# RWKV strips first with block 0's inverse among the other strips, and the GLA heads placed beside block 0's steps

## The chip, the cores and the metric

The kernel runs on one core of a Trainium2 chip. The metric is the device time of one execution in microseconds; a lower time is better. One profiled execution of each kernel gives the trace, in which PE is the matmul engine, DVE, ACT and POOL are the vector, scalar and GpSimd engines, and SP issues most transfers.

## The reference

One block of a diffusion model on 512 latent tokens and 256 context tokens of width 1024. One projection (w_in, 3328 columns) feeds two groups of heads: RWKV-7 (8 heads of 64, both directions) and gated linear attention, GLA (4 heads, both directions). Their outputs go through one projection w_out; an expert-choice mixture of 16 experts follows.

```
proj = h @ w_in
z_rw, z_gla = proj[..., :RW_IN], proj[..., RW_IN:]
z_rw = z_rw + delta_fn(z_rw) * rw_mu                  # token shift: neighbours in the sequence or grid
r, k, v, wd_f, wd_b, ad_f, ad_b, gd = split(z_rw)
g_out = sigmoid(gd) @ rw_g2
y, s = wkv7_scan(r, decay, kk, kk * a, k, v, s0)      # per direction; s <- s*w - (s.kk) kka + v k
rw_out = (group_norm(y_f + y_b) + bonus) * g_out
q, kg, vg, gg, gad_f, gad_b = split(z_gla)
log_a = log_sigmoid(gad @ gla_a2 + gla_a_b) / 16
o = gla_chunked(q, kg, vg, log_a, s0)                 # chunks of 64: b = cumsum(log_a),
                                                      # q*exp(b), k*exp(-b), one state from chunk to chunk
gla_out = rmsnorm(o_f + o_b) * gla_norm_w * silu(gg)
x = ln(ALPHA * x + g1 * (concat(rw_out, gla_out) @ w_out))
x = ln(ALPHA * x + g2 * expert_choice_ffn(modulate(ln(x)), router_w, w_gate, w_up, w_down))
```

## The kernel before

The work is written as Python generators and calls; a scheduler fixes from them, by priorities, one order for each engine, and each engine runs its instructions in that order. Waits on other engines and on transfers are semaphores.

**The strips.** `strip` loads 128 columns of w_in (L287, 512 KB) into one of two buffers `raw`, ACT copies it to `wh` (L289), POOL takes the rest into `wl` (L290). `project` (L298) multiplies with the tokens, three products for each of eight slices of the width (`wh` with `hh`, `wl` with `hh`, `wh` with `hl`). `shifted` adds the token shift. There are 26 strips: gates and GLA keys, queries, values first, then the low-rank strip LT, then blocks of RWKV (k, v and r of a block of two heads; four blocks, 0 to 3).

**GLA.** Per direction and half the decay is computed (L506 to L524). Then 11 chunk steps, each with transposes of the keys (L573, by L45), a copy `kt` (L575), the products with the values (L580) and the state on DVE (L590 to L593). Then scores (L606) and outputs (L627) of eight chunks, four normed heads (L641 to L650) and their write to `og_d` (L651). `feed` hands out strips between the steps.

**Parking w_out.** `park` takes w_out in 16 tiles: a load into `wx` (L554), the product with g1 on DVE (L555), a rounded copy on ACT (L556), the rest on POOL (L557), a write to `wo_d` (L558). `wx` has three buffers, and `ox`, from which the heads are written, has the same tag t3.

**RWKV per block.** `rw_elem` makes the elementwise terms (e_c, e_w, e_i, e_t, matmuls L689, L707, L708); `rw_keys` fills KB and AM (L747 to L751), `rw_scores` multiplies them (L842), `rw_inverse` inverts a triangular matrix for each chunk and head: QD (L866), 15 substitution steps on DVE (L884, L887), block products (L899 to L934), copies into SC (L948, L949). `rw_rho` is L762, `clear` L778. Then 12 steps `rw_step`: the copy of `wt` (L987) on DVE comes once in each step, which needs the state of the step ahead. `rw_post` norms a block's output.

**The order of the blocks before.** All strips and the GLA (53 to 374 us), with block 0's elementwise terms among them. Then scores and inverse of block 0 with `gla_half` (the 96 products L1094 of the GLA heads with their part of w_out, operands `mxg` from `og_d` and `wg` from `wo_d`, loaded on POOL's queue) and block 1's elementwise terms in its gaps. Then block 0's steps, with keys, scores and inverse of block 1 beside them, and so on with the next block. In the first part PSUM has banks d, s and c; behind it w, k, e, i and u.

## Time and profile before

| what | us |
|---|---|
| median of 3 runs (lowest, highest) | 2104.27 (2096.83, 2109.34) |
| the profiled execution, its span | 2105.25, 2103.5 |
| PE busy, DVE, ACT, POOL over the span | 1831.6, 769.4, 481.1, 315.7 |
| strips and GLA | 53 to 374 |
| inverse of block 0, products of the GLA heads | 374 to 437 |
| block 0's steps, keys to inverse of block 1 | 437 to 534 |
| experts | 794 to the end |

The stages are read from the trace; the busy times are of the page. An engine's busy share over the span mixes stages, so the section with rows below cuts the span into windows. A row of a timeline names the start, the duration, the engine, the line, the operation with its tiles, and in brackets the idle time ahead and what ended it.

### The profile page before, as it was taken

Reading aid. Unit: us, or ns where it says so; the run is one execution under the profiler, and the core shown is the slowest. Engines: PE = TensorE matmul, PEld = TensorE weight load, DVE = VectorE, ACT = ScalarE, POOL = GpSimd, SP = SyncE. Lnnn points to the kernel's source line nnn. Section 1 sums busy time; section 2 is a strip of 40 time slices with the busy share of each in tenths; the row PEclk is TensorE's granted clock in tenths of the full one; section 3 lists DMA queues with packets and bytes.
Section 4 is the critical chain, followed back from the end, with each engine's and each line's share of the span. In section 5 each row is a group of like instructions: output and inputs, shape, how many; then the busy total and the mean of one; then the engine's idle time right before and its main releaser. Section 6 shows DMA issues by size and latency. Waiting matters only on the chain. (4 is left out here: it accounts for less than half of the span.)

```text
span 2103.5 us, 31329 instructions
## 1 busy us (share of the span) xinstructions
PE 1831.6 (87%) x13266; PEld 936.1 (44%) x13266; DVE 769.4 (37%) x1445; ACT 481.1 (23%) x978; POOL 315.7 (15%) x318
## 2 busy tenths in 40 slices
PE   5898997788889988999998888988988888889886
PEld 1666776666667653333333333333333332333322
DVE  4676667766663262122112112122122121121113
ACT  2242445555652441011101101010010010011001
POOL 2543656343140220000000000000000000000001
PEclk8989998888897999999999999999999999999998
DMA  7645631510000268999999999999999999999995
GB/s 276 180 147 184 216 102 45 174 46 18 2 28 7 87 269 371 424 424 425 425 425 424 425 425 425 424 425 425 425 425 424 424 425 424 425 424 424 426 424 226
DMA packets 111416, 638.50 MB, mean 304 GB/s; under 512 B 13007, under 2 KB 40248, under 8 KB 60332
## 3 DMA queue, kind: packets, MB, share of 16 engines
q1 hardware_dynamic: 108944, 625.74, 73.1%
q0 software_dynamic: 2016, 10.49, 1.5%
q8 instruction: 104, 1.70, 0.3%
q10 hardware_dynamic: 316, 0.28, 0.0%
q14 instruction: 36, 0.29, 0.0%
HBM read 619.54 MB, written 15.75 MB: 302 GB/s over the span
## 5 line engine op out<-in xcount | busy, mean ns | idle before, releaser
L1446 PE MATMUL ps_gu<-wt,xT 128*64 128x512 f32 (+1 forms) x3072 | 689.2, 568 | 47.7 <-DMA wt<-in_ex_up_dram 35.7
L1446 PEld LDWEIGHTS ps_gu<-wt,xT 128*64 128x64 f32 x3072 | 239.2, 138 | 435.3 <-issue 292.4
L1494 PE MATMUL ps_gu<-wd,hT 128*64 128x512 f32 x1408 | 311.4, 595 | 31.6 <-DMA wd<-in_ex_down_dram 31.6
L1494 PEld LDWEIGHTS ps_gu<-wd,hT 128*64 128x64 f32 x1408 | 97.3, 137 | 233.8 <-issue 173.2
L1467 ACT ACTIVATE gT<-ps_m 128x512 f32<-128x512 f32 x16 | 9.6, 597 | 602.1 <-PE ps_m L45 602.1
L1508 DVE TENSOR_TENSOR ye<-ps_gu,g2b 128x512 f32<-128x512 f32 x16 | 11.1, 692 | 372.1 <-PE ps_gu L1494 372.1
L1297 POOL MEMSET cnt<- 128x12 f32 x16 | 1.6, 107 | 884.8 <-DVE rank L1319 872.7
L1409 PE MATMUL ps_m<-h,oh 128*64 128x512 f32 x256 | 93.1, 615 | 45.9 <-DVE oh L1404 45.9
L1520 DVE TENSOR_TENSOR kx<-kx,ps_m 128x512 f32<-128x512 f32 x120 | 77.1, 684 | 152.0 <-PE ps_m L1514 152.0
L298 PE MATMUL ps_d<-hh,wh 128*128 128x512 f32 (+1 forms) x336 | 127.3, 379 | 4.2 <-ACT kx L362 3.0
L298 PE MATMUL ps_d<-hh,wl 128*128 128x512 f32 (+1 forms) x336 | 122.5, 365 | 5.3 <-POOL wl L290 5.3
L298 PE MATMUL ps_d<-hl,wh 128*128 128x512 f32 (+1 forms) x336 | 123.6, 368 | 3.4 <-POOL hl L269 3.4
L88 DVE TENSOR_SCALAR hm<-hm 128x512 f32<-128x512 f32 (+1 forms) x48 | 19.5, 405 | 180.6 <-ACT hm L1458 180.6
L1411 ACT ACTIVATE xg<-ps_m 128x512 f32<-128x512 f32 x16 | 9.6, 597 | 330.1 <-PE ps_m L1409 330.1
L290 POOL TENSOR_TENSOR wl<-raw,wh 128x1024 fp32r<-128x1024 f32 x26 | 67.4, 2592 | 93.7 <-ACT wh L289 92.8
L1418 DVE TENSOR_TENSOR xT<-ps_m,mod 128x512 f32<-128x512 f32 x16 | 11.1, 692 | 188.5 <-PE ps_m L1414 188.5
L298 PEld LDWEIGHTS ps_d<-hh,wh 128*128 128x128 f32 x336 | 66.9, 199 | 25.8 <-issue 10.1
L298 PEld LDWEIGHTS ps_d<-hh,wl 128*128 128x128 f32 x336 | 67.2, 200 | 15.1 <-POOL wl L290 5.5
L298 PEld LDWEIGHTS ps_d<-hl,wh 128*128 128x128 f32 x336 | 66.9, 199 | 14.3 <-POOL hl L269 5.1
L1514 PE MATMUL ps_m<-ye,gT 64*128 64x512 f32 x244 | 68.8, 640 | 0.0
L1409 PEld LDWEIGHTS ps_m<-h,oh 128*64 128x64 f32 x256 | 28.9, 142 | 85.4 <-issue 77.6
L1303 DVE SCALAR_TENSOR_TENSOR scr<-ps_m,aff,lo 128x128 bf16<-128x128 f32 (+3 forms) x60 | 33.1, 551 | 91.6 <-PE ps_m L1399 90.0
(454 smaller groups left out, 2669.8 us busy)
## 6 DMA issues: line engine op xcount, KB each, us to landing
wt<-in_ex_gate_dram SPq DMA_DIRECT2D x128, 1408.0 KB, 26.4
wt<-in_ex_up_dram SPq DMA_DIRECT2D x128, 1408.0 KB, 27.1
wd<-in_ex_down_dram SPq DMA_DIRECT2D x96, 1536.0 KB, 27.6
wd<-in_ex_down_dram SPq DMA_DIRECT2D x32, 1024.0 KB
adat<-in_ada_w_dram SPq DMA_DIRECT2D x64, 256.0 KB, 3.0
raw<-in_w_in_dram SPq DMA_DIRECT2D x25, 512.0 KB, 3.8
adat<-in_ada_w_dram SPq DMA_DIRECT2D x4, 2048.0 KB
wo_d<-wx SPq DMA_DIRECT2D x16, 512.0 KB, 3.8
```

Of the source, the lines that this page charges most:

```text
L88: V.tensor_scalar(o, o, 1.0, 2.0 ** 60, op0=A, op1=OP.min)
L290: G.tensor_tensor(wl, raw, wh.bitcast(F32), op=S_)
L298: mm(p, a[:, k, :], b[:, k, lo:lo + n], start=k + i == 0, stop=k == KD - 1 and i == 2)
L1303: V.scalar_tensor_tensor(scr[:, l:h], row[:, l:h], aff[:, t, e:e + 1], (lo if before else hi)[:, z + l:z + h], op0=OP.is_ge if before else ...
L1409: mm(p[HR[h]], oh[:, t], h2[t][:, 512 * h:512 * h + 512], start=t == 0, stop=t == 3, skip_group_check=True)
L1411: act(xg, p, AF.Copy)
L1418: V.tensor_tensor(xv, p.rearrange("p (j h s) -> p j h s", j=4, h=2), sc, op=M)
L1446: i = mm(p[HR[h]], xT[:, k], wt[:, h * FH + f0:h * FH + f0 + w], start=k == 0, stop=k == KD - 1, skip_group_check=True)
L1494: mm(py[HR[c]], hT[:, j0 + j, 64 * h:64 * h + 64], wts[h][:, j, 512 * c:512 * c + 512], start=j0 + j + h == 0, stop=j0 + j == 10 and h == ...
L1508: V.tensor_tensor(ye, py, g2b, op=M)
L1514: mm(ps_[c], gT[HR[c], t * P:(t + 1) * P], ye[HR[c]], start=not last, stop=True, skip_group_check=True)
L1520: V.tensor_tensor(x, x, ps_[c], op=A)
```

## The change

- LT's strip comes first, then k, v and r of block 0, then gates, k, v, r of block 1, GLA keys, queries, values and output gates, and k, v, r of blocks 2 and 3. Block 0's elementwise terms, keys, scores and inverse are written among these strips, with banks s and c in place of e and i.
- What the GLA needs (its gate inputs, q, k, v, output gates) and the strips of blocks 2 and 3 are written to DRAM (`zgl_d`, `zq_d`, `zkg_d`, `vg_d`, `sg_d`, `z_d`) and read back later.
- Block 1's elementwise terms, block 0's steps, and the GLA with the parking of w_out are then written one behind the other, and `gla_half` behind these. The GLA's banks are all of kind i, which has two. `wx` and `ox` have two buffers instead of three; g1 has one buffer, loaded anew for each four tiles.
- Keys to inverse of block 1 come behind `gla_half`; the buffers of odd blocks lie where `gla_half` had its tiles.
- `sht`, a buffer of the token shift, is single. Buffers of the steps (wt, VU, kbt, S, SP, sr) get a pool of their own.

The core of the diff:

```diff
+    cur = dict(d=lambda: bank("d", 2), s=lambda: bank("s", 3), c=lambda: bank("c", 3))
+    pd, pss, pc, pe, pi = (lambda n=n: cur[n]() for n in "dscei")
+    cur.update(e=cur["s"], i=cur["c"])
...
     def strips():
+        w = strip([(1536, P)])
+        yield from shifted(w, 12, LT, TC, 0)
...
+        done.add("lora")
+        for n in ("k0", "v0", "r0"):
+            yield from rw_strip(n, dict(k=zk, v=zv, r=zr)[n[0]][0])
...
+        for n in ("k1", "v1", "r1"):
+            yield from rw_strip(n, dict(k=zk, v=zv, r=zr)[n[0]][1])
...
+            q(zkg_d[:, i], z)
...
+        for i, n in enumerate(("k2", "v2", "r2", "k3", "v3", "r3")):
+            z = next(slot)
+            yield from rw_strip(n, z)
+            n = TL if n[0] == "r" else TT
+            nc.sync.dma_start(z_d[:, i, 0:n], z[:, 0:n])
+        done.add("all")
...
+    e = rw_elem(0, pe, fill)
+    for _ in rest:
+        pass
...
+    buffers(0, rpb)
+    rw_keys(0, *e)
+    PC = rw_prep(0, e)
+    until("all")
...
+    cur.update(e=lambda: bankr("e", 2), i=lambda: bankr("i", 2), s=lambda: bankr("i", 2), c=lambda: bankr("i", 2))
...
         def park():
-    wx = gp.tile([P, 3, 2, 512], F32, name="wx", tag="t3")
+            wx = gp.tile([P, 2, 2, 512], F32, name="wx", tag="t3")
...
+                g1 = gp.tile([P, 512], F32, name="g1", tag="ga2")
+                nc.sync.dma_start(g1, mod_d[0, c:c + 1].to_broadcast([P, 512]))
...
-    oxs = gp.tile([P, 3, 2, TL], F32, name="ox", tag="t3")
+        oxs = gp.tile([P, 2, 2, TL], F32, name="ox", tag="t3")
...
-    with after(sub[0]) if O("ea", 1) else contextlib.nullcontext():
-        e = rw_elem(1, pe)
+    e = rw_elem(1, pe)
+    steps(0, PC)
+    gla()
+    c_r2, rp = pool("rw2", "left")
+    late.append(rp)
     with H("glah"):
         gla_half()
     c_rc, rc = pool("rwc", "right")
-    buffers(1)
-    for b in range(4):
-        S = None
-        for s in range(12):
-            S = rw_step(b, s, S, PC)
+    buffers(1, rc)
...
+    for b in range(1, 4):
+        rw_keys(b, *e)
+        PC = rw_prep(b, e)
         if b < 3:
-            rw_keys(b + 1, *e)
-            PC = rw_prep(b + 1, e)
-        if b < 2:
-            e = rw_elem(b + 2, pe)
-        if b == 1:
+            e = rw_elem(b + 1, pe)
+        if b == 2:
             zgs = zp0.tile([P, 3, TL], F32, name="zgs", tag="zkv0")
...
+        steps(b, PC)
```

How this moves instructions, at the places where the prediction has its terms. In after, scores are L650, the inverse L676 to L767, a step's copy of `wt` L1012, the GLA's states L916 to L919, its outputs L953, the sums of squares L968, the parking L883 to L887, the heads' write L976, the products L1106. (A number behind a tile's name counts buffers.)

PE before, from the last strip on: block 0's scores (L842), then products of the GLA heads (L1094) with block 1's elementwise matmuls (L689, L707, L708) and the first of the inverse.

```order
L842 MATMUL ps_e<-AM_2369,KB_2368 128x128 x12
L842 MATMUL ps_e<-AM_2371,KB_2370 128x128 x12
L767 MATMUL ps_e<-e_c,bd_113 128x512
L689 MATMUL ps_e<-e_c,bd_113 128x256
L689 MATMUL ps_e<-e_c,bd_113 128x512
L1094 MATMUL ps_k<-wg,mxg 128x512 x42
L707 MATMUL ps_e<-LS,e_ws 128x256
L708 MATMUL ps_e<-LS,e_ws 128x256
L1094 MATMUL ps_k<-wg,mxg 128x512 x2
L707 MATMUL ps_e<-LS,e_ws 128x512
L1094 MATMUL ps_k<-wg,mxg 128x512
L708 MATMUL ps_e<-LS,e_ws 128x512
```

PE in after, behind the GLA: its last outputs, the heads, all 96 products in a piece (L1106), then block 1's first transposes.

```order
L953 MATMUL ps_i<-qin_3308,sg_3315 128x64 x2
L953 MATMUL ps_i<-zqa,kx_3312 128x64 x2
L968 MATMUL ps_i<-gt,on_3320 128x512 x4
L1106 MATMUL ps_k<-wg,mxg 128x512 x96
L45 MATMUL ps_k<-ident,kx_463 64x128 x4
L994 MATMUL ps_k<-ident,KB_4118 128x128 x2
L994 MATMUL ps_k<-ident,KB_4124 128x128 x2
```

The products left the stage of an inverse and stand by themselves, and block 1's keys and scores follow them.

PE in after, in the middle of the strips: block 0's scores.

```order
L298 MATMUL ps_d<-hh,wh_184 128x512
L298 MATMUL ps_d<-hh,wl_186 128x512
L650 MATMUL ps_s<-AM_1283,KB_1282 128x128 x12
L650 MATMUL ps_s<-AM_1289,KB_1288 128x128 x12
L610 MATMUL ps_s<-e_c,bd_125 128x512
L298 MATMUL ps_d<-hl,wh_184 128x512
L298 MATMUL ps_d<-hh,wh_184 128x512
L298 MATMUL ps_d<-hh,wl_186 128x512
```

Scores (and behind them the inverse) stand between matmuls of strips, where before they came after the last strip.

DVE in after, at the last two steps of block 0 (`wt` is copied once a step) with the first of the parking (L884) and of the GLA's states.

```order
L1042 SCALAR_TENSOR_TENSOR S<-ps_u,PC,SP 128x64 x2
L1072 TENSOR_TENSOR ym<-ym,ps_k 128x2x64
L884 TENSOR_TENSOR wx<-wx,g_3683 128x512
L1012 COPY wt<-ps_w 128x128
L916 TENSOR_TENSOR sg_3314<-ps_i,ebl 128x512
L1072 TENSOR_TENSOR ym<-ym,ps_k 128x2x64
L918 TENSOR_TENSOR sg_3315<-ps_i,sg_3314 128x512
L919 TENSOR_TENSOR sg_3315<-sg_3315,ebl 128x512
L918 TENSOR_TENSOR sg_3315<-ps_i,sg_3315 128x512
L884 TENSOR_TENSOR wx<-wx,g_3683 128x512
L919 TENSOR_TENSOR sg_3315<-sg_3315,ebl 128x512
L884 TENSOR_TENSOR wx<-wx,g_3683 128x512
```

DVE in after, from the last parking products to block 1's keys (L583).

```order
L884 TENSOR_TENSOR wx<-wx,g_3785 128x512
L972 SCALAR_TENSOR_TENSOR og<-gg,cols,gt 128x512 x2
L884 TENSOR_TENSOR wx<-wx,g_3785 128x512 x2
L975 TENSOR_TENSOR ox<-og,ox 128x512 x4
L1135 SCALAR_TENSOR_TENSOR xr<-xr,ps_k 128x512 x8
L583 TENSOR_TENSOR KB_4118<-e_c,e_i 128x12x64
```

Before, all of the parking and the GLA stood ahead of block 0's first copy of `wt`; now 14 of the 16 products of the parking stand behind its last one, ahead of `ox`, and the keys of block 1 behind that.

SP before, the parking's transfers with strips (`raw`) among them.

```order
L558 DMA wo_d<-wx 128x1024 x3
L554 DMA wx<-in_w_out_dram 128x512 x2
L287 DMA raw_174<-in_w_in_dram 128x8x128
L554 DMA wx<-in_w_out_dram 128x512
L558 DMA wo_d<-wx 128x1024 x3
```

SP in after, the same transfers.

```order
L887 DMA wo_d<-wx 128x1024 x2
L883 DMA wx<-in_w_out_dram 128x512 x2
L887 DMA wo_d<-wx 128x1024 x2
L879 DMA g_3717<-mod_d 128x512
L883 DMA wx<-in_w_out_dram 128x512 x2
```

Three writes in a row became two, and no strip stands among them.

## Rows read from the trace of the kernel before

**Rows 1.** Windows: us, busy of each engine with instructions, granted clock, DMA share, GB/s.

```profile
53.00:374.00 321.00, 283.13 (x1795) 219.43 (x1795) 225.75 (x241) 132.95 (x213) 163.71 (x104) 0.93 0.45 143
374.00:437.00 63.00, 51.47 (x844) 39.83 (x843) 40.54 (x74) 36.87 (x53) 19.06 (x22) 0.89 0.50 170
437.00:534.00 97.00, 82.81 (x1442) 64.51 (x1443) 64.70 (x127) 52.03 (x121) 38.17 (x44) 0.83 0.06 18
794.00:2103.00 1309.00, 1150.16 (x5564) 432.95 (x5564) 277.39 (x603) 121.46 (x252) 19.21 (x32) 0.99 0.99 416
```

**Rows 2.** Timeline of PE: start, us, engine, line, instruction; at 73 and 375 us.

```profile
73.19 0.40 PE L298 MATMUL ps_d<-hh,wh 128*128 128x512 f32 x1
73.42 0.40 PE L298 MATMUL ps_d<-hh,wl 128*128 128x512 f32 x1
...
375.36 0.82 PE L842 MATMUL ps_e<-AM,KB 128*128 128x128 f32 x5 [0.42 <-ACT kx L362]
```

**Rows 3.** Page, section 5, over the span: busy us, mean ns, idle before.

```profile
L298 PE MATMUL ps_d<-hh,wl 128*128 128x512 f32 (+1 forms) x336 | 122.5, 365 | 5.3 <-POOL wl L290 5.3
```

**Rows 4.** Timeline of DVE at 480 and 534 us.

```profile
479.46 0.29 DVE L987 COPY wt<-ps_w 128x128 f32<-128x128 f32 x1 [0.16 <-PE ps_w L984]
483.75 0.29 DVE L987 COPY wt<-ps_w 128x128 f32<-128x128 f32 x1 [0.20 <-PE ps_w L984]
...
534.11 0.29 DVE L987 COPY wt<-ps_w 128x128 f32<-128x128 f32 x1
```

**Rows 5.** Windows, 185 to 312 us, of L45, L580, L606 and L627 alone.

```profile
185.00:312.00 127.00, 7.75 (x176) 6.49 (x176) 0.97 0.47 158
185.00:312.00 127.00, 12.65 (x176) 10.09 (x176) 0.97 0.47 158
185.00:312.00 127.00, 4.82 (x128) 4.29 (x128) 0.97 0.47 158
185.00:312.00 127.00, 13.73 (x192) 11.80 (x192) 0.97 0.47 158
```

**Rows 6.** Tile wx: ns min/median/max of one, first and last start.

```profile
L555 DVE TENSOR_TENSOR wx<-wx,g x16: 678/686/1780, 198.2 to 258.0; 128x512 f32<-128x512 f32 x16
L556 ACT ACTIVATE wx<-wx x16: 621/632/635, 199.0 to 259.3; 128x512 fp32r<-128x512 f32 x16
L557 POOL TENSOR_TENSOR wx<-wx x16: 1262/1516/1742, 199.7 to 260.6; 128x512 fp32r<-128x512 f32 x16
...
DMA to landing us min/median/max: 2.6/3.7/5.0
```

**Rows 7.** Page, section 6: DMA issues, KB each, us to landing.

```profile
wo_d<-wx SPq DMA_DIRECT2D x16, 512.0 KB, 3.8
```

**Rows 8.** Timeline of SP around 201 and 212 us.

```profile
201.30 3.25 SPq L558 DMA_DIRECT2D wo_d<-wx  x3
...
212.32 5.03 SPq L558 DMA_DIRECT2D wo_d<-wx  x3
```

**Rows 9.** Lines L641 (first step of a head) and L651 (its write).

```profile
L641 ACT ACTIVATE gt<-og x4: 613/626/632, 293.0 to 301.4; 128x512 f32<-128x512 f32 x4
...
L651 SPq DMA_DIRECT2D og_d<-ox x4: 320/332/345, 301.1 to 308.6; - x4
```

**Rows 10.** Tile mxg, its loads.

```profile
DMA to landing us min/median/max: 5.4/7.3/9.1
```

**Rows 11.** Groups by line, 185 to 312 us, as page section 5.

```profile
L580 PE MATMUL ps_c<-vg,kt 64*64 64x128 f32 x176 | 12.7, 288 | 4.3 <-ACT kt L575 4.2
```

**Rows 12.** Timeline of POOL, keys of block 1.

```profile
436.64 1.79 POOL L747 TENSOR_TENSOR AM<-e_c,e_w 64x756 f32<-64x756 f32 x1 [12.00 <-PE ps_k L1094]
...
449.34 5.58 POOL L762 TENSOR_TENSOR RM<-zr,e_w 64x512 f32<-64x512 f32 x4
```

**Rows 13.** Timeline of ACT, end of inverse 0.

```profile
434.76 0.37 ACT L949 ACTIVATE SC<-ps_i 32x256 f32<-32x256 f32 x1
```

**Rows 14.** Windows, DVE alone, behind block 1's second step.

```profile
534.00:603.00 69.00, 50.45 (x109) 0.94 0.07 21
```

More of the change, by code (lines that the diff above doesn't have):

```diff
@@ L860, in rw_inverse_ @@
         dg = lambda g: SC[j][1 - g // 2][R[g], :, 32 * (g % 2):32 * (g % 2) + 32]
-        QD = rp.tile([P, 32, 32], F32, name="QD", tag="X")
+        if b:
+            QD = late[1].tile([P, 32, 32], F32, name="QD", tag="X")
+        else:
+            QD = rpa.tile([P, 1536], F32, name="QD", tag="e_i")[:, 0:1024].rearrange("p (a b) -> p a b", b=32)
+            big = {n: rpa.tile([P, 1536], F32, name=f"x_{n}", tag=f"e_{n}") for n in "tcw"}
         G.memset(QD[:, :, 24:32], 0.0)
@@ L866, in rw_inverse_ @@
             act(o, i, AF.Copy)
-        gt = kp2.tile([P, 1056], F32, name="gt")
+        gt = late[1].tile([P, 1056], F32, name="gt") if b else big["t"][:, 0:1056]
         g3 = gt[:, 0:1024].rearrange("p (a b) -> p a b", b=32)
@@ L871, in rw_inverse_ @@
         busy(gt[:, 0:32], O("b1",(0,0))[b>0])
-        X = rp.tile([P, 1056], F32, name="X")
+        X = late[1].tile([P, 1056], F32, name="X") if b else rpa.tile([P, 1536], F32, name="X", tag="e_i")[:, 0:1056]
         G.memset(X, 0.0)
@@ L880, in rw_inverse_ @@
                 n, m = 15 - s, s + 1
[L881 removed]
+                tmp = late[1].tile([P, 128], F32, name="xtmp", bufs=1) if b else big["t"][:, 1056:1184]
                 tv = tmp[:, 0:2 * n * m].rearrange("p (i a b) -> p i a b", i=2, b=m)
```

579 lines of the change are left out of this document (285 added, 294 removed).

## The prediction

> **What bounds the kernel now.** I first cut the span at the places where the kind of work changes and read the busy time of each engine there [rows 1]. The last 1309 us, the experts, move 416 GB/s with the DMA engines 0.99 busy, and the change touches nothing there. All that it moves lies between 53 and 603 us. From 53 to 374 us PE is busy 283.1 of 321 us with the strips and the GLA: at their densest the strips' matmuls, 512 wide, stand 0.23 us apart [rows 2], and the granted clock is 0.93. The idle is 38 us in all, of it 5.3 us ahead of matmuls that wait for a strip's split on POOL [rows 3]. From 374 to 437 us the bound is another: the inverse of block 0 is a chain of small steps over four engines, and its gaps hold the 96 GLA products and block 1's elementwise work. From 437 to 534 us block 0's steps (4.3 us each where nothing is in the way [rows 4]) run beside the inverse of block 1; 534.1 us is block 1's second step, which needs that inverse. From block 1's steps on the order of after is that of before, so I take the time from there to the end as it is, and ask when block 1's second step comes.
>
> **The strips, 53 to 374 us.** Out go the GLA chain and outputs, 7.75 + 12.65 + 4.82 + 13.73 = 39 us of PE [rows 5], and the sums of squares of the four heads (4). In come scores, rho and inverse of block 0. Their PE work is bounded by the stage in which they now stand, 51.5 us busy [rows 1] less 96 products at 0.23, so at most 29; block 1's elementwise matmuls are among that too, and I take 17. Busy then is 283 - 43 + 17 = 257. Idle was 38; the inverse's small matmuls stand in order among the strips' and can hold them up, but some 400 matmuls follow it with nothing in the way, and the waits of the GLA chain are gone: 21. That makes 278, against 321, a gain of 43 us; its bounds are 252 (all idle gone) and 300 (idle and lost clock as now, and some 5 of new stalls). The some twenty new writes to DRAM (GLA inputs, late strips) go beside this, with the DMA share at 0.45 [rows 1], and cost nothing as long as that holds; if not, they are in the upper bound.
>
> **The stage 374 to 437 us falls out of the way ahead of block 0's steps.** That is what the change buys: at 53 + 278 = 331 us the first step can begin. Beside the steps stand now elementwise work of block 1 and the gates, by my sum over the order of after, with the durations that the same instructions have in the trace, some 47 us of DVE and 51 of ACT; twelve free steps take 52. I take 60 (52 to 68), so they end at 391.
>
> **What now stands behind block 0's steps.** This is the term that decides. In the order of DVE two of the 16 parking products (L884) and the first GLA state stand ahead of block 0's last copy of wt; the 14 others, ten GLA states, the outputs and the heads stand behind it. Four chains hang on each other there.
> - Parking. One tile is a load, a DVE product (0.69), an ACT copy (0.63), a POOL subtraction (1.5) and a write; a load lands after 3.7 us [rows 6], a write after 3.8 [rows 7], and the queue of the writes shows rounds of three buffers 11 to 12 us apart [rows 8]. With two buffers a round (the two buffers' loads, work and writes in a row on SP's queue) is 3.7 + 0.7 + 0.6 + 1.5 + 3.8 = 10.3 at the least, with the second tile's POOL 11.8; I take 11. The first pair's products stand some 6 us before the last step ends, so the eighth pair's are at -6 + 7 x 11 = +71 us after the steps, and its writes have landed at +78.
> - The heads. ox takes the buffer of wx (one of the tag t3), so its first ACT copy waits for the last write of the parking. Before, four heads followed each other in 293.0 to 308.6 us [rows 9]; their squares, roots and products with the gate now hide behind the parking, and what is left is two pairs of copy, subtraction, write: 2 x (2 + 3.8) = 12, so og_d is whole at +90.
> - The products. mxg and wg are loaded behind that on POOL's queue and landed after 7.3 us (5.4 to 9.1) [rows 10]; the 96 products then come in one piece, 96 x 0.233 = 22.4, since nothing of an inverse is left to pair them with. Before, the same 96 lay in the gaps of inverse 0 and cost that stage little. End: +90 + 7.3 + 22.4 = +120.
> - The GLA chain itself is 39 us of PE, and 45 with waits like the 4.2 us for kt that it had before [rows 11]; it hides beside the parking.
>
> I take 120, so 391 + 120 = 511. Bounds: 130 with rounds of 12.4, and 94 if the parking bounded nothing (45 + 15.6 for the heads + 3.8 for the last write + 7.3 + 22.4).
>
> The Trainium skill (DMA: Bandwidth & Descriptors, Anatomy of one DMA — SWDGE (gpsimd) path) gives a DMA of POOL's queue a fixed 2 us and the bytes at 436 GB/s; an estimate by that page for one of the loads of 1 MB is 4.4 us, and the sum would be 3 us less. The row says 7.3, for loads that share the engines, and the sum goes by the row.
>
> **Keys, scores and inverse of block 1.** Their buffers lie where the products' tiles are, so they begin behind them. Before, POOL's part (AM, clearing, RM) took 436.6 to 454.9 us [rows 12], 18 us, with nothing else needing it soon; now the scores wait for the AM part of it. From inverse 0's first scores (375.4 [rows 2]) to its last copy (434.8 + 0.4 [rows 13]) are 60 us, with elementwise work beside it as now. 18 + 60 = 78, and 2 for the keys, scores and elementwise work of block 2 that stand among them: 80 (68 if the scores start before POOL is through, 97 if it runs as inverse 1 did before, from 454.9 to 534). Block 1's second step is then at 511 + 80 = 591, where it was 534.1: +57. In the 69 us behind it DVE was busy 50.5 [rows 14]; elementwise work, keys and scores of block 2, some 14 of these, now stand ahead, which is between 0 and 14 us less for the steps: -6. The late strips that come back from DRAM are asked for while the parking runs, long before they are used.
>
> **The sum.** -43 (strips) - 62.5 (inverse stage) - 97 (the stage to 534) + 60 + 120 + 80 = +57.5, less 6: +51 us. On the profiled execution's 2105.25 us (span 2103.5) that is 2156; it stands 1 us above the median of the runs, so 2155.
>
> **Rivals.**
> 1. The parking does not bound: rounds of two buffers hide beside the GLA chain, the heads follow it directly. For it: the chain has work for 45 us, and SP's queue has nothing else of weight. Against it: seven rounds are 77 us even at 11, and 72 at the least. Price -26, 2129. Chance 0.15. The Trainium skill (Trainium Kernel Development and Optimization, Best Practices) asks for two buffers so that DMA and compute overlap, and by that rule this would be the case; the rows, in which a load and a write together are 7.5 us [rows 6, 7] against 1.5 us of the slowest engine, speak against two being enough.
> 2. The strips gain little: the inverse's small matmuls, in order on PE, make the strips wait, and the clock falls. Then the strips take 300 or more and the time is 2177 to 2185. For it: the clock of 0.83 in the stage 437 to 534 [rows 1], where such matmuls stand among others; against it: there the big matmuls that could fill were missing. Chance 0.17.
> 3. The other side: the GLA and the parking really run beside block 0's steps, as the words of the change have it. Then behind the steps only the last pair of heads, loads and products are left, 6 + 7.3 + 22.4, some 36 to 45 instead of 120, and the time is 2155 - 75 = 2080. It decides if the parking's last write has landed by the end of the steps. Against it: an engine runs its instructions in order, and on DVE 14 of 16 products of the parking stand behind the last wt copy. It would need steps that themselves wait so long that all else has caught up. Chance 0.06.
> 4. Smaller gains pile up (strips at their lower bound, scores 1 ahead of POOL's end, parking hidden): 2155 - 26 - 26 - 12 = 2091 at the very most, and about 2105 where each comes halfway or more: no change. Chance 0.06.
>
> The forecast itself (2132 to 2176) has 0.56. About 10 us either way, 0.5%, is what a measurement of this kernel can tell from no change. Range: from rival 1's lower side to rival 2's upper side, 2112 to 2186. Faster by more than 0.5%: rival 3 and the best of 4, 0.08. The same: the rest of 4 and the best of 1, 0.08. Slower: 0.84.
>
> **What the profile of after would show.** Strips end near 331 us with the wt copies of block 0 from there to 391. After the last one, PE mostly idle for 100 us but for the GLA chain, with DVE's L884 in pairs 11 us apart, its wait named as the DMA of wx; ox waiting for wo_d; then L1106 in one block of 22 us near 490 to 511; L650 of block 1 some 10 to 18 us later; block 1's second wt near 591; and from there the same distances as before. Wrong would be: L1106 within 50 us of the last step (rival 3), L884 without DMA waits (rival 1), strips that end past 353 (rival 2), or a tail from block 1's second step to the end that isn't the 1570 us of before less a few.

## The result: 7% slower, three times the predicted loss

The changed kernel takes 2252.9 us in the median (2245.4 to 2256.5), the kernel before 2102.5 in the same comparison: a ratio of 1.071 (95% interval 1.067 to 1.075). Predicted were 2155 us and at most 2186. The direction held, the size did not: the span of the profiled execution grew by 146.6 us (2103.5 to 2250.1), not by 51.

The table cuts both traces at the same events: the first and the last copy of `wt` of block 0, the start of the last of the GLA products, the second copy of `wt` of blocks 1, 2 and 3. (In the kernel before the products lie ahead of block 0's steps.)

| stretch | before | predicted | after | after less predicted |
|---|---|---|---|---|
| start to block 0's first step | 440.1 | 331 | 349.7 | +18.7 |
| block 0's steps | (with inverse 1) 94.0 | 60 | 79.7 | +19.7 |
| to the last GLA product | - | 120 | 136.6 | +16.6 |
| to block 1's second step | - | 80 | 98.8 | +18.8 |
| to block 2's second step | 77.1 | 71 | 92.4 | +21.4 |
| to the end | 1492.2 | 1492.2 | 1492.9 | +0.7 |

There is no single step that went wrong. Five terms were each too small by 17 to 21 us, and the last 1493 us came out as predicted.

Windows of the changed kernel, to be set against [rows 1] of before (us; busy time and instructions of PE, its weight loads, DVE, ACT and POOL; granted clock, DMA share, GB/s):

```profile
53.00:347.00 294.00, 248.53 (x1823) 198.25 (x1821) 177.69 (x205) 118.33 (x181) 127.52 (x81) 0.92 0.41 122
350.00:430.00 80.00, 63.44 (x606) 44.23 (x606) 39.25 (x80) 48.76 (x106) 24.90 (x22) 0.55 0.15 49
430.00:566.00 136.00, 77.67 (x770) 63.61 (x766) 42.68 (x59) 24.76 (x46) 28.90 (x26) 0.71 0.58 201
566.00:665.00 99.00, 54.58 (x880) 41.33 (x878) 64.01 (x89) 39.43 (x61) 35.10 (x34) 0.62 0.06 20
665.00:757.00 92.00, 80.90 (x1323) 60.19 (x1324) 50.90 (x108) 46.94 (x111) 23.58 (x27) 0.69 0.06 16
```

The third number from the end, the granted clock of TensorE as a share of full speed, is the first thing to see. Before, the stages behind the strips ran at a granted clock of 0.89 and 0.83, and [rows 4] show block 0's steps at 4.3 us; now the four stretches behind the strips have 0.55 to 0.71. The cuts themselves, on DVE of the changed kernel (start, duration, line, instruction, idle time ahead and what ended it):

```profile
349.70 0.29 DVE L1012 COPY wt<-ps_w 128x128 f32<-128x128 f32 x1 [0.41 <-PE ps_w L1003]
...
423.59 0.68 DVE L884 TENSOR_TENSOR wx<-wx,g 128x512 f32<-128x512 f32 x1
429.39 0.29 DVE L1012 COPY wt<-ps_w 128x128 f32<-128x128 f32 x1 [0.58 <-PE ps_w L1009]
...
566.39 0.69 DVE L1135 SCALAR_TENSOR_TENSOR xr<-xr,ps_k 128x512 f32<-128x512 f32 x1 [0.25 <-PE ps_k L1106]
...
664.81 0.27 DVE L1012 COPY wt<-ps_w 128x128 f32<-128x128 f32 x1
```

Row by row: block 0's first `wt`, the first parking product, block 0's last `wt`, the last accumulation behind the GLA products, block 1's second `wt`. The parking's first product stands 5.8 us ahead of the last `wt`, as the order had it (predicted: 6).

**In the strips.** Two of PE's four longest waits between 53 and 347 us (total, times, longest):

```profile
PE ps_c L715 <- DVE x_c L704: 9.3, 1, 9.3
...
PE ps_s L650 <- POOL AM L621: 6.7, 1, 6.7
```

Both are new: the inverse's products and block 0's scores stand in order among the strips' matmuls, in the middle of a strip, and PE waits for DVE and POOL before it goes on with that strip. PE was idle for 45 us of the 294, where 21 were predicted (and 38 were there before); it was busy 248.5 us, 8.5 less than predicted.

**In block 0's steps.** ACT between the third and the fourth step (`VU`, L1020 and L998, are copies of the step; the other rows shown are elementwise terms of block 1):

```profile
363.43 0.83 ACT L84 ACTIVATE e_w<-e_w 128x768 f32<-128x768 f32 x1
...
366.72 1.02 ACT L559 ACTIVATE e_c<-e_t,der,cols 128x768 f32<-128x768 f32 x1
367.64 0.83 ACT L563 ACTIVATE e_w<-e_i 128x768 f32<-128x768 f32 x1
368.49 0.27 ACT L1020 ACTIVATE VU<-ps_u 64x128 f32<-64x128 f32 x1
...
374.04 0.27 ACT L998 ACTIVATE VU<-ps_k 64x128 f32<-64x128 f32 x1
```

The third step's `wt` is at 360.8 us and the fourth's at 378.1. In between the step needs three short copies of ACT; it gets them at 368.5, 370.8 and 374.0, behind runs of terms of up to 1.03 us each.

**Behind them.** SP's queue, with the parking's loads (L883) and writes (L887) and the heads' writes (L976):

```profile
431.26 2.86 SPq L883 DMA_DIRECT2D wx<-in_w_out_dram  x2
...
441.91 4.42 SPq L883 DMA_DIRECT2D wx<-in_w_out_dram  x2
...
453.55 4.79 SPq L883 DMA_DIRECT2D wx<-in_w_out_dram  x2
...
510.63 1.54 SPq L887 DMA_DIRECT2D wo_d<-wx  x2
516.01 5.73 SPq L976 DMA_DIRECT2D og_d<-ox  x4
```

The first rounds are 10.7 and 11.6 us long, against 11 predicted; the four behind them take 11.8 to 12.6. The last writes go out 82 us behind block 0's last step, and `ox` can be filled at +85, when they have landed; predicted was +78. This step was right but for some 7 us. In the changed kernel the heads' copy waits for that write (first row); in `halfpark`, a run below that leaves out half of the parking, it waits for DVE's product of the heads (second row):

```profile
514.63 1.15 ACT L974 ACTIVATE ox<-og 128x512 fp32r<-128x512 f32 x2 [4.75 <-DMA wo_d<-wx]
```

```profile
495.97 0.63 ACT L978 ACTIVATE ox<-og 128x512 fp32r<-128x512 f32 x1 [0.46 <-DVE og L976]
```

Then POOL's queue, from the heads' transfers to block 1's keys:

```profile
520.63 0.72 POOL L1121 DMA_DIRECT2D mxg<-og_d  x1 [8.81 <-DMA og_d<-ox]
...
529.86 0.53 POOL L1121 DMA_DIRECT2D mxg<-og_d  x1 [7.98 <-DMA og_d<-ox]
530.38 1.06 POOL L1122 DMA_DIRECT2D wg<-wo_d  x2
...
550.01 0.54 POOL L1122 DMA_DIRECT2D wg<-wo_d  x1 [18.25 <-PE ps_k L1106]
566.44 1.78 POOL L590 TENSOR_TENSOR AM<-e_c,e_w 64x756 f32<-64x756 f32 x1 [15.89 <-PE ps_k L1106]
...
574.11 6.62 POOL L605 TENSOR_TENSOR RM<-zr,e_w 64x512 f32<-64x512 f32 x4
...
582.90 3.07 POOL L621 MEMSET AM<- 64x768 f32 x4
```

The second `mxg` waits until 529.9 us for the heads' last write, the two loads of `wg` behind it wait with it, and the last waits for a buffer of the products. The loads of `wg` landed after 6.3 to 11.7 us, 10.1 in the median, while three loads of late strips that SP issues between 523.0 and 529.8 us are under way. From the heads' last landing (529.9 us) to the last product it is 36 us instead of the predicted 7.3 + 22.4. The products come in four pieces, of which these are the second and the last:

```profile
540.22 13.77 PE L1106 MATMUL ps_k<-wg,mxg 128*128 128x512 f32 x48 [3.81 <-DMA wg<-wo_d]
...
560.61 5.73 PE L1106 MATMUL ps_k<-wg,mxg 128*128 128x512 f32 x24 [1.21 <-DVE xr L1135]
```

The first 60 of them took 0.29 to 0.38 us each, at a granted clock of 0.69 (531 to 540 us) and 0.73 (540 to 550); the last 36 took 0.24 to 0.25, at 1.00. The 96 filled PE for 27.0 us instead of 22.4, and the waits of PE ahead of and between them are 9.5 us instead of 7.3. So more of the loss is in the products than in the landing of their operands. And from the last product (566.4) POOL works 19.5 us on AM, RM and the clearing of both before the scores can begin. Before, the clearing of AM stood ahead of RM; here it stands behind it.

**In inverse 1.** DVE in the substitution steps (L697, L700), and one row of POOL; L378 and L560 are terms of block 2:

```profile
607.73 0.28 DVE L697 TENSOR_TENSOR xtmp<-gt,X 128x120 f32<-128x120 f32 x1
607.93 1.75 DVE L378 TENSOR_TENSOR_SCAN e_i<-smask,e_w 128x768 f32<-128x768 bf16 x1
609.60 0.26 DVE L700 TENSOR_TENSOR X<-X,xtmp 128x120 f32<-128x120 f32 x1
609.88 1.80 POOL L560 TENSOR_TENSOR e_c<-e_c,kx 128x768 f32<-128x768 f32 x1 [6.57 <-issue]
609.89 1.94 DVE L697 TENSOR_TENSOR xtmp<-gt,X 128x126 f32<-128x126 f32 x1
```

The 30 instructions, 0.2 to 0.3 us each where nothing holds them up, took from 602 to 632 us; in the run `held2`, without that work, from 602.6 to 611.2. Other work between them is one part. Another is that six of the 30 took 1.2 to 1.9 us themselves, 9.4 us together, and all six began while POOL ran terms or keys of block 2, as in the last two rows. In `held2` POOL stands still during the steps and none of them takes over 0.3 us. Not every step beside POOL was longer, and no run takes POOL's part away by itself, so that its price of some 8 us is a reading of the trace.

### The profile page after: what moved, and what is told of

It is laid out like the page before. It is cut to its first block, busy times and chain, and to the rows that moved or that the text cites. A ratio compares the mean times of both kernels' runs of the same rounds, so it can differ in the third digit from the quotient of the medians.

```text
span 2250.1 us, 31414 instructions
## 1 busy us (share of the span) xinstructions
PE 1876.2 (83%) x13258; PEld 971.8 (43%) x13258; DVE 762.0 (34%) x1435; ACT 488.2 (22%) x988; POOL 307.0 (14%) x318
## 5 line engine op out<-in xcount | busy, mean ns | idle before, releaser
L1521 PE MATMUL ps_gu<-wd,hT 128*64 128x512 f32 x1408 | 311.2, 595 | 28.2 <-DMA wd<-in_ex_down_dram 28.1
L1535 DVE TENSOR_TENSOR ye<-ps_gu,g2b 128x512 f32<-128x512 f32 x16 | 11.1, 692 | 368.5 <-PE ps_gu L1521 368.5
L1436 PE MATMUL ps_m<-h,oh 128*64 128x512 f32 x256 | 96.2, 628 | 45.7 <-DVE oh L1431 45.7
L1547 DVE TENSOR_TENSOR kx<-kx,ps_m 128x512 f32<-128x512 f32 x120 | 77.1, 684 | 152.7 <-PE ps_m L1541 152.7
L298 PE MATMUL ps_d<-hh,wh 128*128 128x512 f32 (+1 forms) x336 | 122.6, 365 | 5.2 <-ACT hh L268 1.5
```

The source lines that it names most:

```text
L298: mm(p, a[:, k, :], b[:, k, lo:lo + n], start=k + i == 0, stop=k == KD - 1 and i == 2)
L1436: mm(p[HR[h]], oh[:, t], h2[t][:, 512 * h:512 * h + 512], start=t == 0, stop=t == 3, skip_group_check=True)
L1521: mm(py[HR[c]], hT[:, j0 + j, 64 * h:64 * h + 64], wts[h][:, j, 512 * c:512 * c + 512], start=j0 + j + h == 0, stop=j0 + j == 10 and h == ...
L1535: V.tensor_tensor(ye, py, g2b, op=M)
L1547: V.tensor_tensor(x, x, ps_[c], op=A)
```

## The experiments

Each is one edit with one run, beside one of the kernel before on the same chip (2107.7 to 2122.3 us there). All runs of the kernel before lie between 2096.8 and 2122.3 us, so a total is good to some 10 us either way, and what is compared is mostly stretches of the traces, cut as above:

| run | first step | block 0's steps | to last product | to block 1's second | to block 2's second | span |
|---|---|---|---|---|---|---|
| before | 440.1 | 56.8 | - | 37.2 | 77.1 | 2103.5 |
| split | 440.4 | 47.0 | - | 76.8 | 80.1 | 2133.3 |
| after | 349.7 | 79.7 | 136.6 | 98.8 | 92.4 | 2250.1 |
| warm_steps | 354.4 | 83.9 | 127.9 | 100.6 | 105.6 | 2274.1 |
| warm_light | 355.4 | 85.1 | 136.7 | 95.5 | 96.2 | 2261.1 |
| alone | 353.4 | 42.6 | 199.8 | 96.8 | 82.9 | 2268.1 |
| elem_early | 376.6 | 67.3 | 136.0 | 98.2 | 83.0 | 2253.8 |
| halfpark | 359.6 | 78.8 | 116.0 | 99.1 | 92.2 | 2238.2 |
| held2 | 354.1 | 78.7 | 133.7 | 81.6 | 90.1 | 2242.8 |
| rmlate | 358.4 | 81.9 | 133.7 | 90.6 | 82.9 | 2240.4 |
| early_rm | 376.0 | 67.2 | 136.1 | 92.8 | 91.7 | 2256.5 |
| inv0fill | 494.2 | 79.7 | 135.9 | 99.3 | 92.4 | 2394.0 |

(In `pair` and `pair_early` the order of the stages is another; their numbers are below.) The two theories at the start: A, that the half clock makes the stages long; B, that the steps share ACT and DVE with work that is in their way and the clock is a by-product.

**split: block 0's steps alone, in the kernel before.** Block 1's keys to inverse and the terms of block 2 may only be issued behind block 0's last `wt`.

```diff
-        if b < 3:
-            rw_keys(b + 1, *e)
-            PC = rw_prep(b + 1, e)
...
+        with after(wts[11]) if b == 0 else contextlib.nullcontext():
+            if b < 3:
+                rw_keys(b + 1, *e)
+                PC = rw_prep(b + 1, e)
...
```

> The kernel before, with one edit: keys, scores, inverse of block 1 and elementwise work of block 2 may only be issued after block 0's last copy of wt, so that block 0's steps run with nothing beside them, as they nearly do in the changed kernel. Theory A (what cost the changed kernel most is the clock: a chain of steps without an inverse beside it leaves PE at the half clock, and each step grows): the granted clock in block 0's steps falls from 1.00 to 0.5 to 0.6, a step takes 5.5 to 6.5 us instead of 4.3 to 4.5, block 1's second step comes at 605 to 620 us instead of 534, and the time is 2175 to 2190. Theory B (the clock is a by-product; the steps of the changed kernel are long because elementwise work of block 1 and the GLA gates share DVE and ACT with them): steps stay at 4.3 to 4.7 us, the second step of block 1 comes at 570 to 585 and the time is 2140 to 2157.

Neither theory's numbers came. Block 1's second step is at 564.1 us (A had 605 to 620, B 570 to 585), and the time is 23.6 us above the run beside it. The lone steps took 47 us, less than beside an inverse. But the half clock that A is about is there. PE during the steps, in stretches of 10 us:

```profile
450.00:460.00 10.00, 7.65 (x99) 0.50 0.01 2
460.00:470.00 10.00, 10.00 (x101) 0.52 0.01 2
470.00:480.00 10.00, 9.77 (x145) 1.00 0.01 2
```

At the half clock (450 to 470 us) the `wt` copies of these steps are 5.1, 5.1, 5.8 and 5.1 us apart, at the full one (470 to 487 us) 4.0, 4.0, 4.0 and 3.7. So the half clock costs a lone step about 1.2 us, 14 for twelve; by itself it does not make 80 us of 47. Keys to inverse of block 1 by themselves took 77 us.

**warm_steps and warm_light: idle products on PE in each step.** Four (the diff), and then one (only the last line, with 1), of 32 x 384 that nobody reads:

```diff
+    def warm(b, dep, n):
+        for _ in range(n if b < 2 else 0):
+            mm(wbk[0:32, P:512], dep, KB[b][0][:, 0:3, :].rearrange("p c t -> p (c t)"), start=True, stop=True,
+               skip_group_check=True)
...
+            warm(b, wt[:, 0:32], 2)
...
+                warm(b, VU[:, 0, 0:32], 2)
```

> The changed kernel with four idle products on PE (32 x 384, into a part of a PSUM bank that nobody reads) in each step of blocks 0 and 1: two that read the step's wt and two that read its VU. They add about 0.5 to 0.65 us of PE each and nothing else. Theory A: the granted clock between 350 and 430 us rises from 0.57 to 0.9 or more, the twelve steps of block 0 take 60 to 66 us instead of 80, block 1's 59 go to 52 to 56, and the time is 2220 to 2235 instead of 2250. Theory B: the clock rises but the steps take as long or longer, since PE has more to do, and the time is 2250 to 2275.

> The changed kernel with one idle product (32 x 384) in each step of blocks 0 and 1, behind the state's products, where PE waits for DVE; four of them, in the run warm_steps, gave PE the full clock but so much work that the steps did not gain. If the half clock costs a step 1.2 us, as the lone steps of the run split show (5.1 to 5.8 us at 0.5, 4.0 at 1.0), and one product is enough to keep the clock: block 0's steps take 66 to 72 us instead of 80, block 1's 50 to 54 instead of 59, the time is 2225 to 2238. If the queues of ACT and DVE set the steps whatever the clock: 78 to 84 us, and 2250 to 2262. If the granted clock stays below 0.7 there, the run tells nothing of either.

```profile
347.00:430.00 83.00, 76.34 (x633) 0.98 0.19 62
```

```profile
355.00:440.00 85.00, 72.81 (x626) 0.66 0.14 44
```

With four (first row) the granted clock was 0.98 and the steps took 83.9 us, as B had it; but PE was busy 76 us of the window's 83, some 43 of them with matmuls that are not the steps' own, so its own queue may have set them. With one (second row) the clock stayed at 0.66: by its own condition this run tells nothing. The clock can't be separated in this way, since what holds it up costs PE as much as it gives.

**alone: the terms of block 1 and the GLA held back until block 0's steps are through, in the changed kernel.**

```diff
-    e = rw_elem(1, pe)
     steps(0, PC)
-    gla()
+    with after(wts[11]):
+        e = rw_elem(1, pe)
+        gla()
```

> The changed kernel with elementwise terms of block 1 and the GLA (gates first) held back until block 0's last copy of wt, so that nothing but the last strip stands beside block 0's steps. In the run split the lone steps took 47 us, 5.1 to 5.8 us each at the half clock and 3.7 to 4.0 at the full one. Theory C (block 0's 80 us are long since ACT and DVE have the elementwise terms and the gates in their queues ahead of the steps' copies, and the half clock adds about 1.2 us a step): the steps take 47 to 55 us; what is held back comes behind them and takes 25 to 45 us before the first GLA state, so the time is 2240 to 2265, about that of the changed kernel. Theory A (the clock alone makes them long): the steps take 62 to 75 us even with nothing beside.

```profile
353.00:396.00 43.00, 37.71 (x564) 28.75 (x564) 12.64 (x45) 15.60 (x59) 3.99 (x10) 0.92 0.21 74
396.00:562.00 166.00, 70.65 (x726) 52.83 (x724) 69.45 (x93) 59.29 (x96) 50.42 (x35) 0.60 0.36 123
```

The twelve steps took 42.6 us, less than either theory had. So 37 of the 79.7 us come from what stands beside them, together with the clock that fell with it. The traces divide them. The steps' own 558 matmuls fill PE for 37.3 us here, at a clock of 0.92, and for 50.9 us in the changed kernel, at 0.55: 13.6 us go with the clock, as much as `split` gave. The 40 matmuls of terms, gates and GLA among them fill 14.6 us there, of which 2.4 overlap with the steps' own. And PE is idle for 16.6 us of the steps instead of 5.3: 11 us of waits, the longest of them for ACT's copies. The three parts were read off, not taken away one by one.

What was held back came behind the steps: the first GLA state stands 64 us behind the last `wt`, not 25 to 45, so that sharing is still the better order: 80 us for both, against 43 + 64.

**elem_early: only the gates beside the steps.** The terms of block 1 are written behind inverse 0, among the last strips.

```diff
     PC = rw_prep(0, e)
+    until("rwr1")
+    e = rw_elem(1, pe, fill)
     until("all")
...
-    e = rw_elem(1, pe)
     steps(0, PC)
```

> The changed kernel with the elementwise terms of block 1 written behind inverse 0, among the last strips, instead of beside block 0's steps; the gates stay beside the steps. From 250 to 347 us ACT and DVE have little to do, so the terms should be hidden there. Theory C (what stands in ACT's and DVE's queues ahead of the steps' copies makes the steps long; alone they take 42.6 us, with terms and gates 80): with the gates only they take 55 to 65 us and the time is 2225 to 2238. Theory A (the half clock is most of it): 70 to 78 us, since the gates bring no PE work that keeps the clock, 2240 or more.

```profile
376.00:444.00 68.00, 60.16 (x602) 40.73 (x604) 28.07 (x69) 33.74 (x83) 20.99 (x19) 0.60 0.17 56
```

The steps took 67.3 us, between the two expectations: of the 37 us the terms make 12 and the gates 25, each with what it does to the clock. The two shares are of different kinds. With the gates alone PE is idle for 7.8 us of the steps, hardly more than in `alone`; what grows is its busy time, 48.3 us of the steps' own matmuls (0.60 of the clock) and 13.5 of others. The terms add 9 us of idle time. The kernel before shows the same steps beside an inverse:

```profile
440.00:497.00 57.00, 49.61 (x700) 37.93 (x698) 41.66 (x100) 36.32 (x83) 21.71 (x31) 0.91 0.06 16
```

DVE and ACT had more to do there in less time (41.7 and 36.3 us, against 28.1 and 33.7), and the other work on ACT is as long by the single instruction in both (a median of 0.83 us); and yet the steps took 56.8 us. The clock there is 0.91, at which the steps' own matmuls fill 36.0 us of PE.

And nothing was won in the total, since the first step came 27 us later. The terms were not hidden among the strips; they stand ahead of the strips' copies and of the inverse, and PE waits for these:

```profile
PE ps_c L715 <- DVE x_c L704: 18.6, 1, 18.6
PE ps_d L298 <- ACT ym L450: 11.5, 1, 11.5
```

**pair: the GLA ahead of block 0's steps, these beside inverse 1.**

```diff
-    steps(0, PC)
     gla()
...
+    steps(0, PC)
     for b in range(1, 4):
         rw_keys(b, *e)
```

> The changed kernel with block 0's steps written behind the GLA and the products instead of ahead of them, so that they run beside keys, scores and inverse of block 1 as in the kernel before; strips, parking and all else as in the changed kernel. Theory A: the steps get their clock back (0.8 or more from the first step of block 0 to the second of block 1, where the changed kernel has 0.57 and 0.62 in two stretches), the stretch from the last product to block 1's second step is 95 to 105 us, about what it was without the steps in it, and the time is 2170 to 2195. Theory B: steps and inverse share DVE (41 and 63 us of it in the changed kernel) and PE, so that the stretch is 125 to 150 us and the time 2200 to 2240.

```profile
347.00:400.00 53.00, 20.12 (x45) 0.60 0.27 86
...
551.00:610.00 59.00, 52.73 (x629) 0.91 0.08 20
610.00:654.00 44.00, 33.50 (x846) 0.77 0.05 15
```

The stretch from the last product (548.2 us) to block 1's second step (653.4) is 105 us at a clock of 0.91 and 0.77, as A had it, with the steps inside it (58.7 us beside the inverse, as before's 56.8). Clock and company came back together here, so this run does not tell them apart. But the total is 2234 (span 2232.1), where B had it: between the strips' end (350.8 us) and the first GLA state (413.8 us) terms and gates stand bare (first row: PE busy 20 of 53 us). `pair_early`, the diffs of `pair` and `elem_early` together, was to take the terms away from there:

> The run pair (GLA and products ahead of block 0's steps, these beside keys to inverse of block 1; 2234) with the elementwise terms of block 1 among the last strips. If what kept pair from gaining was that terms and gates stood bare between the strips and the GLA chain, 15 to 25 us go: 2208 to 2220. It would stay slower than the kernel before by some 100, since the GLA with its parking, heads and products is bare in it: from the strips' end to the last product nothing else needs PE. If the gates were the longer chain there, 2225 to 2234.

It took 2243 us, above both expectations. The stretch from the strips' end to the first GLA state fell from 63 to 49 us, but the strips ended 17.5 us later (368.3 us), and the first of the products L1106 came 5 us later than in `pair` (519.3 against 514.1 us). What the terms left behind was lost again in the strips, as in `elem_early`.

**halfpark: half of the parking left out.** Eight of the 16 tiles (those of the RWKV half) go to `wo_d` as they are, without product and split.

```diff
+                    if k >= 4:
...
+                    else:
+                        q(wo_d[c, :, k, 0], wo[:, k, 512 * c:512 * c + 512])
+                        q(wo_d[c, :, k, 1], wo[:, k, 512 * c:512 * c + 512])
```

> The changed kernel with eight of the 16 tiles of w_out (those of the RWKV half) left out of the parking: they are copied as they are from DRAM to DRAM, without the product with g1 and the split, so the RWKV half of the output projection is wrong. Theory P (the parking is what the heads wait for, as the prediction had it): og_d is whole 20 to 25 us earlier and the time is 2225 to 2232. Rival (the GLA's chain and outputs, at the half clock, end hardly earlier than the parking): og_d is whole at most 10 us earlier, 2240 or more.

```profile
507.11 3.14 SPq L980 DMA_DIRECT2D og_d<-ox  x2
```

The heads' last write goes out at 510 us instead of 521, while block 0's last step was 9 us later (438.3): from there to the last product it was 116.0 us instead of 136.6. With eight tiles the parking's last write goes out at 473 us and no longer bounds: `ox` waits for DVE there (the rows of `ox` above). So the parking is what the heads wait for in the changed kernel, and that costs 20.6 us, where rival 1 had 26. The total missed its range (2225 to 2232): it came out at 2240, which is the other theory's, by the 10 us that the first step was later.

**held2: the terms of block 2 held back until inverse 1's substitution is through.**

```diff
-            e = rw_elem(b + 1, pe)
+            with after(sub[0]) if b == 1 else contextlib.nullcontext():
+                e = rw_elem(b + 1, pe)
```

> The changed kernel with elementwise terms of block 2 (and so its keys and scores) held back until the substitution steps of inverse 1 are through on DVE. The prediction gave 2 us for all that stands among inverse 1. If it is more than that, since DVE runs them in order between the substitution steps (the 30 instructions of those take from 602 to 632 us, some 17 of it other work), block 1's second step comes 12 to 18 us earlier behind the last product, 80 to 87 us instead of 98; the work then stands beside block 1's steps and these take 5 to 15 us longer, so the time is 2240 to 2252. If it was hidden, the 98 us stay, and the time is 2255 to 2265.

From the last product to block 1's second step 81.6 us instead of 98.8: 17 us of the prediction's "2". They were given back for the most part in block 2's steps (from block 2's second step to block 3's 97.9 us instead of 86.0), not in block 1's, as was expected (90.1 us instead of 92.4).

**rmlate: the RM products behind the clearing.** One number of the kernel's table of priorities, that of block 1's rho (cut out of the table's one long line):

```diff
-h_rho=(0, 500, 60, 400)
+h_rho=(0, -500, 60, 400)
```

> The changed kernel with one number of the table changed: rho of block 1 loses its priority, so that on POOL the four RM products (6.6 us) stand behind the clearing of AM instead of ahead of it. If the scores of block 1 wait for POOL's clearing, as the trace names it, block 1's second step comes 5 to 7 us earlier behind the last product and the time is 2243 to 2247. If another wait ends at the same time, nothing moves, 2250 to 2253.

The stretch to block 1's second step fell by 8.2 us (98.8 to 90.6), a little more than the 5 to 7 expected for a wait of the scores on POOL. What was not expected is block 1's steps:

```profile
665.00:714.00 49.00, 43.60 (x719) 30.80 (x720) 35.07 (x86) 33.54 (x80) 10.91 (x14) 0.92 0.04 13
```

Between block 1's second step and block 2's, PE has the same 1324 matmuls in `rmlate` as in the changed kernel, and DVE, ACT and POOL run the same instructions in the same order; and yet the time to block 2's second step is 82.9 us here and 92.4 there. The granted clock is 0.92 here; in the changed kernel it is 0.68 (665 to 724 us).

**early_rm: the diffs of elem_early and rmlate together**, to see whether that was luck.

> elem_early and rmlate together. If the two prices are of different waits they add up: 2215 to 2228, with the granted clock in block 1's steps at 0.9 or more as in rmlate and 49 to 52 us for them. If rmlate's gain in block 1's steps (59 to 49 us for the same instructions) was luck of the clock, those take 55 us or more again and the time is 2228 to 2238.

It was. With the same instructions again, the time to block 2's second step is 91.7 us, at a clock of 0.74 from 672 to 730 us. In seven runs of these same instructions it was 82.9, 82.9 and 83.0 (`rmlate`, `alone`, `elem_early`) or 91.7, 92.2, 92.4 and 92.4 (`early_rm`, `halfpark`, `inv0fill`, after). The steps also fall behind exactly where the clock is at its lower level: in the changed kernel between 672 and 703 us, where it has 0.50 until 702; in `early_rm` by 0.9 us until 684, where it has 0.50 until 682, and by the rest from 709 us on, when it falls to 0.50 again (until 736). Here, then, is the price of the clock: 9.5 us of a stage of 83. The total, 2258, again has the later strips of `elem_early` in it.

**inv0fill: inverse 0's small products one by one between the strips' matmuls**, by its priority in the same table (cut out in the same way).

```diff
-h_inv=(200, 0, 0, 100)
+h_inv=(-600, 0, 0, 100)
```

> The changed kernel with one number of the table changed: inverse 0 loses its priority, so that its small products on PE stand one by one between the strips' matmuls, where in the changed kernel they stand in blocks and PE waits 9.3 us for the first of them and 6.7 us for the clearing ahead of the scores. If these in-order waits are why the strips ended some 15 us later than predicted, the first step of block 0 comes at 335 to 342 us instead of 350, and the time is 2236 to 2243. If the strips' own loads and splits take the place of the waits, 347 to 355 us and 2248 to 2258.

The wait for `x_c` was gone, as meant, and the first step came at 494 us: 144 us later, with every later stretch as in the changed kernel. PE alternates between a strip's matmul and a pair of small products (timeline; then the window 350 to 450 us):

```profile
400.20 0.31 PE L737 MATMUL ps_c<-x_w,WD 32*32 32x32 f32 x2
400.44 0.80 PE L298 MATMUL ps_d<-hh,wl 128*128 128x512 f32 x1
...
401.40 0.80 PE L298 MATMUL ps_d<-hl,wh 128*128 128x512 f32 x1
...
350.00:450.00 100.00, 100.00 (x382) 0.50 0.07 21
```

A 512-wide matmul with a pair of small products behind it takes 0.96 us, where two 512-wide ones stood 0.23 us apart [rows 2] and a small one in a block cost PE 0.015 us (155 of them in 2.3 us, from 240.7 us on, in the changed kernel). Part of that is the clock: it stays at 0.50 although PE counts as busy all the time. At the full clock, from 262 to 266 us of the same run, a 512-wide matmul with its pair took 0.59 us. The first step missed both expectations by some 140 us or more. So whether the in-order waits alone made the strips late is not settled: the edit that took them away put something worse in their place.

## Why the prediction was wrong, by its own steps

**What was right.** The largest term (what stands behind block 0's steps, 137 us) and that it is read from the order of DVE, the mechanism of the parking with its rounds of 11 to 12 us and the heads that wait for it, the keys of block 1 behind the products, and that the stages from block 2 on stay as they are. `halfpark` shows rival 1's price (20.6 us against 26). Rival 3, the GLA really beside the steps, did not happen: the first product of the 96 came 102 us behind the last step.

**The strips, 278 us.** The mis-sized part is the idle time, 45 us instead of 21; the busy time was 8.5 us less than the 257 of the sum. I had given the waits of the GLA chain as gone and nothing for those of the inverse but a bound; the trace names 9.3 + 6.7 us of these. That is rival 2's mechanism, its waits without its clock (0.92 in the strips), at more than half of its price. That the strips would have gained these 16 us without the waits is argued: `inv0fill` was to show it and did not. The lower bound, 252 with "all idle gone", was a slip, since it lies below the busy time. In the runs that leave the strips alone the first step comes at 349.7 to 359.6 us, so the profiled run is the best of them. The rest is open.

**Block 0's steps, 60 us.** The step that failed is "twelve free steps take 52. I take 60": it gave 8 us to the beside-work, as filling holes, and bounded the sum by the busiest engine (51 us of ACT). It put PE, and the clock, at nothing. Free steps take less than 52 (42.6 to 47.0 us); with gates and terms beside them they took 79.7. Shown is that these 37 us come with the beside-work (`alone`, `elem_early`). By the traces some 14 of them go with the clock, which fell from 0.92 to 0.55, some 12 are the matmuls of the beside-work in PE's own order, and 11 are waits, since each copy of the chain waits until what stands ahead of it in the queue of ACT or DVE is through. How the clock would have held without the matmuls, or the waits without the clock, no run shows.

**The tail, 120 us.** Mis-sized by 16.6: the parking 7, the heads 3, and 6.5 in the loads and products. In the parking the rounds grew to some 12 us; loads of the heads' gates and of the late strips stand in SP's queue among the later ones, but that they are the cause isn't shown. In the last part 4.6 us are the products themselves, taken at 0.233 us each and run at 0.28 in the mean, with the first 60 at a granted clock of 0.69 to 0.73; 2 are waits, mostly for `wg`, whose last load waited for a buffer. That the late strips are asked for "while the parking runs, long before they are used" was right; that they go beside the `wg` loads was missed (that these land late for it is argued from the trace, not tested).

**Keys to inverse of block 1, 80 us.** The step that failed is "and 2 for the keys, scores and elementwise work of block 2 that stand among them". The 60 us were taken from inverse 0 "with elementwise work beside it as now". But inverse 0 had its terms held back by the kernel's own `after(sub[0])`, a line that the diff takes out (they began on DVE at 402.8 us, where the substitution had ended); it stood in the quoted diff and I didn't price it. `held2`, which puts such a line back, measures it: 17 us. The 18 us on POOL were nearly right (19.5), and `rmlate` shows that 8 of them need not have been waited for, with the clearing ahead of RM as it was before.

**Block 1's steps, -6 us.** Here the sign was wrong. I had only counted work that leaves the stage; the stage's clock went from 0.95 (534 to 611 us before) to 0.69 (665 to 757 us). 9.5 of the 21 us are that, by the seven runs of the same instructions; the stage at a clock of 0.92 takes 83 us, still 6 more than before's 77, where 6 less were predicted.

**The range.** Each term had bounds, but the range was set as if one or two of them would be missed at a time. They were missed together. What they share, as far as the runs show it, is that every duration came from a stage with other company and, for three of the five at least, another clock: an estimate from the figures above is that the lower clock makes some 28 of the 95 us (14 in block 0's steps, 4.6 in the products, 9.5 in block 1's). The waits in the strips, the rounds of the parking and the line that held the terms back are causes of their own.

No version here beats the kernel before. The best, `pair`, `rmlate` and `halfpark` (the last with work left out), have spans 129 to 137 us above its 2103.5. In all of them the GLA with its parking, heads and products has nothing beside it that needs PE for long; that this is the reason was not tested.

## What to carry to other kernels

When a change moves work beside a chain, don't bound the sum by the busiest engine. Ask of each engine, PE included, what stands in order ahead of the chain's next link, and at which clock the chain will run. The same twelve steps took 42.6 us alone at a clock of 0.92, 56.8 beside an inverse at 0.91, 67.3 beside gates at 0.60 and 79.7 beside gates and terms at 0.55; neither the busy time of DVE and ACT nor the length of their single instructions puts these in order. When a change takes a chain and its cover apart, price both again, and look up the granted clock of each stretch that a price comes from: the same instructions took 83 us at 0.92 and 92 at 0.7. Read what the removed lines of a diff held back, since one of them was worth 17 us. And if all terms of a sum come from stages that the change takes apart, let the range hold their sum, not the worst one of them.

## What the runs showed of the hardware that I had not expected

- The same instructions have two times, by the clock that they are granted: seven runs of block 1's steps fell into 82.9 to 83.0 and 91.7 to 92.4 us, with nothing between. In the changed kernel the lower level lasts from 655 to 702 us, in `rmlate` from 659 to 672, in `early_rm` from 661 to 682 and again from 709 to 736. What decides between them isn't shown.
- With single small products (32 x 32, in pairs) between its 512-wide matmuls PE had a granted clock of 0.50 from 350 to 450 us of `inv0fill` (0.53 from 260 to 450 us) while it counted as busy throughout, and each 512-wide matmul with its pair took 0.96 us, against 0.59 at the full clock. In the changed kernel, where these products come in blocks and the strips behind them, it was 0.98 (250 to 347 us).
- Short instructions of DVE took much longer beside work of POOL: a substitution step of 0.29 us took 1.94 us from 609.89 us on, beside a product of POOL from 609.88 to 611.68 us. Six of the 30 took 1.2 us or more, and none in `held2`, where POOL stood still.
